# A two-layer encoder on one core: which pairs take seven products, what is loaded first, and how the last block ends

## The chip, the cores and the metric

The kernel runs on one core of one Trainium2 chip. The metric is device time in microseconds of one execution, the median of the runs.

## The reference, cut to what matters

Two layers. Each reads the RMS-normalised input through one input projection, runs grouped-query attention with a rotary embedding beside a bidirectional retention, gates both, and adds an output projection to the residual. A final RMSNorm follows.

```python
D_MODEL = 4096; SEQ = 256; DEPTH = 2
for l in range(DEPTH):
    h = rmsnorm(x, norm_w[l])
    proj = h @ w_in[l]                       # (256, 4096) @ (4096, 11264)
    aq, ak, av, ag, rq, rk, rv, rg = jnp.split(proj, SPLIT_POINTS, axis=-1)
...
    a_out = (jax.nn.silu(ag) * gqa_attention(aq, ak, av)).astype(x.dtype)
...
    r_out = (jax.nn.silu(rg.astype(jnp.float32)) * r).astype(x.dtype)
    x = x + jnp.concatenate([a_out, r_out], axis=-1) @ w_out[l]     # (256, 4096) @ (4096, 4096)
return rmsnorm(x, final_norm)
```

## The kernel before

**Blocks and pairs.** The two projections of each layer are cut into blocks of 1024 output columns: 11 blocks of w_in, then 4 of w_out, 15 a layer, numbered 0 to 29 over both. Blocks 11 to 14 and 26 to 29 are the w_out of the two layers. Within a block the 4096 inputs are taken as 16 pairs of 128-row tiles. Two rows of tokens (m = 0, 1) by two halves of columns is a 2x2 matrix product for each pair, and it is done either with eight plain products (EIGHT_PRODUCTS, L182) or with seven (SEVEN_PRODUCTS, L171, a Strassen-Winograd form). The products of all pairs gather in PSUM banks M1 to M7.

**Products.** Every fp32 operand is split in a high and a low part, and one product is three matmuls of 512 columns: high by high, low by high, high by low. Only pairs 0 and 1 of block 0 are multiplied as plain fp32 (NATIVE), since there the input isn't split yet.

**Parts.** A weight page (pair and letter A, T, B or U) is loaded by SP (tile wraw); ACT writes its high part (whi) and DVE its low part (wlo). For a pair with seven products DVE also makes two weight sums (wsum) and both engines split them (pages T and U). "Far" pages (FARS, L101) take another way: POOL's queue loads the high part (fhi), ACT negates it (flo), and a second, adding DMA makes the low part. The stationary operands are the activations' parts: x7h and x7l for pairs that have seven parts, x8h, x8l and x3 for the others.

**Which pairs.** sevens_of() (L207) gives the pairs with seven products of a block: those in SEVEN, and those in AFTER from a given block on. slots_of() (L236) writes out the products of each page; a T or U page of a pair with eight products has none. A pair that changes to seven between blocks is converted by sevenfold() (L1105).

**Order.** The order of pages on PE is written by hand in ORDERS (L87) for some blocks, else in_groups() (L218) makes it. The order on ACT, DVE, POOL and SP is made when the program is built, by a planner (pump, L1344, and aside, L1377) that picks by due times; SETS (L110) gives single blocks other slacks. Once built, each engine runs its own list in order.

**The start.** SP loads `small` (gains and decays), the half of x for pair 1 (tile `full`), two halves of pair 1's weights (`fhi`), and the other half of x. ACT scales x by the gains (split_pair, L998), first index 0, then 1. PE multiplies 20 times on zeros (warm, L2163) ahead of that.

**The end.** In the last block pair 15's products stand last, in the order M5, M2, M3, M4 (FINAL_ORDER), and M4 has 30 matmuls at the end, ten products of five pairs. last_combine() (L2059) adds the banks into `ca` and `cb` (two column blocks, rows m = 0 and 1), adds the residual (`res`, in tiles x8h and x8l), squares and sums. When a row's sum is there, POOL takes the power (tile `last`), ACT and DVE scale the eight column blocks of the row, and SP stores each (tile to `out`, 256 KB). Row 0 is done after M3, row 1 after M4.

## Time and profile before

| | |
|---|---|
| median of 3 runs | 2579.61 us (2579.35 to 2580.07) |
| the profiled execution, its own time | 2581.24 us |
| its span, first to last instruction | 2579.4 us |
| TensorE busy | 2565.5 us, 99% |
| VectorE busy | 2347.1 us, 91% |
| ScalarE busy | 1695.7 us, 66% |
| GpSimd busy | 461.3 us, 18% |
| DMA | 688.64 MB, mean 267 GB/s |

The profiled execution lies 1.63 us above the median, and 1.84 us of its time lie outside the span. Times below are us from the start of the span. PE is TensorE, DVE is VectorE, ACT is ScalarE, POOL is GpSimd, SPq is SyncE's queue. A matmul's own duration overlaps the next one; how far two starts lie apart is what it costs.

### The profile page before, as it was taken

The page shows a single profiled execution, that of the slowest core. Times are in us where ns is not written, and L with a number is a line of the kernel's source. Part 1 is how long each engine was busy: PE and PEld are TensorE (multiplying, and loading weights), DVE is VectorE, ACT ScalarE, POOL GpSimd, SP SyncE. Part 2 cuts the span into 40 slices and gives each one's busy share as a digit, 9 for nine tenths or more (in the row PEclk, how much of TensorE's full clock was granted, in tenths as well). Part 3 has the DMA queues.
Part 4 walks back from the last instruction along what each step waited for, and adds up shares of the span by engine and source line. Part 5 has one row for each costly group of instructions (what it writes and reads, how often), then busy time and mean ns, then how long its engine had stood idle before and what let it go on. Part 6 is the DMA issues. An engine that isn't in the chain of part 4 may idle for free.

```text
span 2579.4 us, 34271 instructions
## 1 busy us (share of the span) xinstructions
PE 2565.5 (99%) x11491; PEld 2124.7 (82%) x11491; DVE 2347.1 (91%) x2951; ACT 1695.7 (66%) x2439; POOL 461.3 (18%) x682
## 2 busy tenths in 40 slices
PE   9999999999999999999999999999999999999998
PEld 6888888888888888888888888888888888888886
DVE  7998998999989999888999998989999899998887
ACT  7766676666655668555786666776676566675565
POOL 0112221221111111221221112212211111111111
PEclk9999999999999999999999999999999999999999
DMA  9988988888778787998998889888987787888886
GB/s 329 318 265 267 290 260 271 287 273 254 228 237 263 226 287 236 294 279 245 326 310 261 270 260 298 276 258 284 275 264 232 239 254 239 276 245 265 265 269 204
DMA packets 198401, 688.64 MB, mean 267 GB/s; under 512 B 24272, under 2 KB 24400, under 8 KB 198224
## 3 DMA queue, kind: packets, MB, share of 16 engines
q1 hardware_dynamic: 126160, 445.24, 48.4%
q0 software_dynamic: 72064, 241.21, 37.1%
q8 instruction: 90, 1.47, 0.2%
q14 instruction: 87, 0.71, 0.1%
HBM read 639.17 MB, written 47.19 MB: 266 GB/s over the span
## 4 chain that ended last, share of the span: by engine, by line
PE 98%; DVE 1%; DMA 1%; issue 0%; ACT 0%; POOL 0%; POOLq 0%; DVEq 0%; SPq 0%; ACTq 0%
PE M L446 94%; PE ps L446 4%; DMA q<-q_dram 0%; DVE wlo L446 0%; DVE cb L446 0%; DMA full<-in_xT 0%; ACT ps L446 0%; DVE ca L446 0%; ACT whi L446 0%; ACT pTh L446 0%; ACT full L446 0%; DVE aql L446 0%; DVE sgT L446 0%; POOLq L2288 0%; DVE wsum L446 0%
## 5 line engine op out<-in xcount | busy, mean ns | idle before, releaser
L446 ACT CAST whi<-wraw 128x1024 fp32r<-128x1024 f32 (+1 forms) x811 | 756.5, 938 | 358.6 <-PE M L446 296.4
L446 DVE TENSOR_TENSOR wlo<-wraw,whi 128x1024 fp32r<-128x1024 f32 (+1 forms) x811 | 866.3, 1078 | 68.7 <-ACT whi L446 63.4
L446 ACT CAST whi<-wsum 128x1024 fp32r<-128x1024 f32 x406 | 426.2, 1050 | 252.7 <-PE M L446 122.2
L446 DVE TENSOR_TENSOR wlo<-wsum,whi 128x1024 fp32r<-128x1024 f32 x406 | 494.5, 1218 | 103.2 <-ACT whi L446 73.7
L446 PE MATMUL M<-whi,x7h 128*128 128x512 f32 x1465 | 570.7, 390 | 0.0
L446 PE MATMUL M<-whi,x7l 128*128 128x512 f32 x1465 | 570.4, 389 | 0.0
L446 PE MATMUL M<-wlo,x7h 128*128 128x512 f32 x1465 | 475.9, 389 | 0.0
L446 PE MATMUL M<-whi,x8l 128*128 128x512 f32 x1165 | 453.5, 389 | 0.0
L446 PE MATMUL M<-whi,x8h 128*128 128x512 f32 x1165 | 453.5, 389 | 0.0
L446 PE MATMUL M<-wlo,x8h 128*128 128x512 f32 x1165 | 359.7, 389 | 0.0
L446 PEld LDWEIGHTS M<-wlo,x7h 128*128 128x128 f32 x1465 | 275.1, 188 | 57.3
L446 PEld LDWEIGHTS M<-whi,x7l 128*128 128x128 f32 x1465 | 275.2, 188 | 56.4 <-issue 0.2
L446 PEld LDWEIGHTS M<-whi,x7h 128*128 128x128 f32 x1465 | 275.2, 188 | 56.3 <-issue 0.2
L446 PEld LDWEIGHTS M<-wlo,x8h 128*128 128x128 f32 x1165 | 218.7, 188 | 45.5
L446 PEld LDWEIGHTS M<-whi,x8h 128*128 128x128 f32 x1165 | 218.8, 188 | 45.2 <-DVE ca L446 0.2
L446 PEld LDWEIGHTS M<-whi,x8l 128*128 128x128 f32 x1165 | 218.8, 188 | 44.9
L446 ACT ACTIVATE flo<-fhi 128x1024 fp32r<-128x1024 f32 (+1 forms) x145 | 152.2, 1050 | 155.8 <-PE M L446 150.6
L446 DVE TENSOR_TENSOR wsum<-wraw 128x1024 f32<-128x1024 f32 x203 | 247.0, 1217 | 4.7 <-PE M L446 2.8
L446 PE MATMUL M<-whi,x 128*128 128x512 f32 x736 | 226.7, 389 | 0.0
L446 POOL DMA_DIRECT2D fhi<-in_w_in x106 | 58.8, 555 | 865.3 <-PE M L446 865.1
L446 PE MATMUL M<-fhi,x8l 128*128 128x512 f32 x429 | 167.0, 389 | 0.0
L446 PE MATMUL M<-fhi,x8h 128*128 128x512 f32 x429 | 167.0, 389 | 0.0
(266 smaller groups left out, 3172.4 us busy)
## 6 DMA issues: line engine op xcount, KB each, us to landing
wraw<-in_w_in SPq DMA_DIRECT2D x594, 512.0 KB, 5.9
wraw<-in_w_out SPq DMA_DIRECT2D x217, 512.0 KB, 6.3
fhi<-in_w_in POOLq DMA_DIRECT2D x106, 512.0 KB, 5.1
flo<-in_w_in POOLq DMA_DIRECT2D x106, 512.0 KB, 8.2
fhi<-in_w_out POOLq DMA_DIRECT2D x36, 512.0 KB, 4.7
flo<-in_w_out POOLq DMA_DIRECT2D x36, 512.0 KB, 8.3
full<-next_dram POOLq DMA_DIRECT2D x24, 512.0 KB, 7.6
p_dram<-room POOLq DMA_DIRECT2D x64, 128.0 KB, 5.2
```

Source lines behind the costliest of these rows:

```text
L446: op.call()
```

## The change

- SEVEN loses pair 2, and AFTER gains it: from block 0 on in the first layer's w_in and in both w_out, from the second block on in the second layer's w_in. So in block 15 pair 2 takes eight products where it took seven, and sevenfold() converts it for block 16.
- EXTRA is (4,). Neither SEVEN nor AFTER names pair 4, and sevens_of() reads nothing else, so pair 4 has eight products in every block, as before; the pages 4T and 4U in the new orders have no product. The code in sevenfold() that puts parts in the rotary tables' tile (`cs`) is there before and after and isn't reached.
- The hand-written orders of blocks 1, 6, 10, 11, 12, 15, 24, 26, 27, 28 and 29 differ in what they yield (blocks 1 and 15 fall back to in_groups()); of the other 19 blocks the order on PE is what it was. Blocks 0 and 12 have other far pages, three fewer in all. Some planner settings differ.
- At the start x goes ahead of `small`, and index 1 of x is scaled before index 0.
- In the last block row 0's additions go first. Row 1's M5 addition and its residual move behind M3. The last two products of M4 are done in two column halves, the second into a bank of its own ("rest"), with an addition and a square for each.

Over the whole program PE has 9 more matmuls: three of 512 columns, and twelve of 256 in the place of six of 512. DVE has 4 more instructions, ACT 1, SP 3 more loads of wraw, POOL 6 fewer DMAs.

SP, the start of the program. Before:

```order
L446 DMA small_97<-in_small 128x128
L446 DMA full_128<-in_xT 128x512
L446 DMA fhi_130<-in_w_in 128x512 x2
L446 DMA full_128<-in_xT 128x512
L446 DMA fhi_134<-in_w_in 128x1024
```

After:

```order
L458 DMA full_127<-in_xT 128x512
L458 DMA small_97<-in_small 128x128
L458 DMA fhi_130<-in_w_in 128x512 x2
L458 DMA full_127<-in_xT 128x512
L458 DMA fhi_134<-in_w_in 128x1024
```

`small` and the first half of x have changed places; the rest stands.

PE, first block of the second layer (15), pair 2: page A before (its pages T, B and U follow further on, 21 matmuls in all):

```order
L446 MATMUL M1_11721<-whi_11775,x7h_11436 128x512
L446 MATMUL M1_11721<-whi_11775,x7l_11437 128x512
L446 MATMUL M3_11737<-whi_11775,x7h_11436 128x512
L446 MATMUL M3_11737<-whi_11775,x7l_11437 128x512
L446 MATMUL M1_11721<-wlo_11782,x7h_11436 128x512
L446 MATMUL M3_11737<-wlo_11782,x7h_11436 128x512
```

Page A after (with page B, which follows, 24 matmuls):

```order
L458 MATMUL M3_11737<-whi_11787,x7h_11437 128x512
L458 MATMUL M3_11737<-whi_11787,x7l_11438 128x512
L458 MATMUL M5_11749<-whi_11787,x7h_11437 128x512
L458 MATMUL M5_11749<-whi_11787,x7l_11438 128x512
L458 MATMUL M4_11756<-whi_11787,x7h_11437 128x512
L458 MATMUL M4_11756<-whi_11787,x7l_11438 128x512
L458 MATMUL M2_11759<-whi_11787,x7h_11437 128x512
L458 MATMUL M2_11759<-whi_11787,x7l_11438 128x512
L458 MATMUL M3_11737<-wlo_11797,x7h_11437 128x512
L458 MATMUL M5_11749<-wlo_11797,x7h_11437 128x512
L458 MATMUL M4_11756<-wlo_11797,x7h_11437 128x512
L458 MATMUL M2_11759<-wlo_11797,x7h_11437 128x512
```

The pair feeds M3, M5, M4 and M2 in place of all seven banks, with three matmuls more.

DVE, the end of the last block, from the additions after bank M6 to the first scaling of an output. Before (x8h and x8l are the residual's rows 1 and 0; `last` is the sum of row 0):

```order
L446 TENSOR_TENSOR cb_23017<-ca_23016,x8h_22650 128x512
L446 TENSOR_TENSOR ca_23016<-ca_23016,x8h_22646 128x512
L446 TENSOR_TENSOR cb_23017<-cb_23017,x8l_22648 128x512
L446 TENSOR_TENSOR ca_23016<-ca_23016,x8l_22644 128x512
L446 TENSOR_TENSOR cb_23017<-cb_23017,M5_22470 128x512 x2
L446 TENSOR_TENSOR ca_23016<-ca_23016,M2_22482 128x512
L446 TENSOR_TENSOR cb_23017<-cb_23017,M3_22459 128x512
L446 TENSOR_REDUCE last_23111<-sums_20250 128x1
L446 TENSOR_SCALAR last_23111<-last_23111 128x1
L446 TENSOR_SCALAR cb_20978<-cb_20978,last_23111 128x512
```

After:

```order
L458 TENSOR_TENSOR cb_23033<-cb_23033,x8l_22625 128x512
L458 TENSOR_TENSOR ca_23032<-ca_23032,x8l_22621 128x512
L458 TENSOR_TENSOR cb_23033<-cb_23033,M5_22464 128x512
L458 TENSOR_TENSOR ca_23032<-ca_23032,M2_22491 128x512
L458 TENSOR_TENSOR cb_23033<-cb_23033,M3_22458 128x512
L458 TENSOR_TENSOR cb_23033<-ca_23032,M5_22464 128x512
L458 TENSOR_REDUCE last_23098<-sums_20249 128x1
L458 TENSOR_SCALAR last_23098<-last_23098 128x1
L458 TENSOR_TENSOR cb_23033<-cb_23033,x8h_22627 128x512
L458 TENSOR_TENSOR ca_23032<-ca_23032,x8h_22623 128x512
L458 TENSOR_SCALAR cb_20975<-cb_20975,last_23098 128x512
```

Two residual additions and one of the two M5 additions have moved behind M3; the two residual additions now stand between row 0's mean and its first scaling.

The diff, cut to its core (of the tables a line or two):

```diff
--- before.py
+++ after.py
@@ -66,13 +66,13 @@
-SEVEN = (0, 2, 5, 8, 11, 13)
+SEVEN = (0, 5, 8, 11, 13)
...
-AFTER = ({10: (3, 1)}, {10: (1, 1)})
-EXTRA = ()
+AFTER = ({2: (0, 1), 10: (3, 1)}, {2: (0, 0), 10: (1, 1)})
+EXTRA = (4,)
@@ -85,34 +85,42 @@
 ORDERS = {
...
-    12: '0A 0T 1A 0B 1B 0U 2A 3A 2T 3B 2B 4A 2U 4B 5A 6A 5T 6B 5B 7A 5U 7B 8A 9A 8T 9B 8B 8U 10A 10T 10B 10U 11A 12A 11T 12B 11B 11U 13A 14A 13T 14B 13B 13U 15A 15B',
...
+    12: '0A 0T 1A 1B 0B 0U 2A 3A 2T 3B 2B 2U 4A 4T 4B 5A 4U 6A 5T 6B 5B 7A 5U 7B 8A 9A 8T 9B 8B 8U 10A 10T 10B 10U 11A 12A 11T 12B 11B 11U 13A 14A 13T 14B 13B 13U 15A 15B',
...
 FARS = {
-    0: '3B 9B 12B 15B 7A',
+    0: '3B 15B 10A',
...
 SETS = {
-    (0, 'PE_REST'): 6.0,
+    (0, 'PE_REST'): 2.0,
...
+    (6, 'PE_REST'): 4.0,
...
-    (10, 'SOFT'): 5.0,
+    (11, 'PE_REST'): 4.0,
+    (11, 'SLACK'): 1.0,
...
+    (27, 'REST'): 4.0,
@@ -249,6 +257,10 @@
+LAST_SOME = NB // 2
+LAST_ENTRIES = 2
@@ -637,7 +649,6 @@
-    sy.dma_start(small, small_in)
@@ -778,13 +789,15 @@
-        def load_whole(self, n):
+        def load_whole(self, n, k=ALL):
...
+            if k == 0:
+                sy.dma_start(g.raw[:, 0, :], g.src[0][:, 0, :])
+                return
...
-            for k in (1, 0) if n == 0 else (ALL,):
-                sy.dma_start(g.raw[:, k, :], g.src[0][:, k, :])
+            sy.dma_start(g.raw[:, k, :], g.src[0][:, k, :])
@@ -1004,7 +1017,7 @@
         if gains:
-            for i in range(2):
+            for i in (1, 0):
@@ -1847,7 +1860,7 @@
         def combining():
-            for _ in range(len(first)):
+            for _ in range(len(first) + last):
                 while not events:
@@ -1919,10 +1932,11 @@
-        def multiply(name, a, b, start, stop):
+        def multiply(name, a, b, start, stop, cols=ALL):
...
+            b, to = b[:, cols], acc[name][:, cols]
...
-            op.e, op.ins, op.outs, op.dma = "P", ins, [region(acc[name])], None
+            op.e, op.ins, op.outs, op.dma = "P", ins, [region(to)], None
@@ -1930,7 +1944,7 @@
-            pe.matmul(acc[name], a, b, start=start, stop=stop)
+            pe.matmul(to, a, b, start=start, stop=stop)
@@ -1948,10 +1962,10 @@
-        n = 0
-        while n < len(flat):
+        n, until = 0, len(flat) - (LAST_ENTRIES if last else 0)
+        while n < until:
             group = [(n, *flat[n])]
-            while n + len(group) < len(flat) and (flat[n + len(group)][1], flat[n + len(group)][3]) == (flat[n][1], flat[n][3]) and len(group) < TOGETHER:
+            while n + len(group) < until and (flat[n + len(group)][1], flat[n + len(group)][3]) == (flat[n][1], flat[n][3]) and len(group) < TOGETHER:
@@ -1975,6 +1989,21 @@
             n += len(group)
+        end = [(m, *flat[m]) for m in range(until, len(flat))]
+        end = [(m, p, k, h, stationary(p, index), prepare(name, p, index, k, h)) for m, name, p, index, k, h in end]
+        if end:
+            acc["rest"] = t(pm, [P, NB], "M1")
+        for name, cols in (("M4", slice(0, LAST_SOME)), ("rest", slice(LAST_SOME, NB))) if end else ():
+            for i, (m, p, k, h, a, g) in enumerate(end):
+                final_one = i == len(end) - 1
+                for j in range(2):
+                    multiply(name, a[j], g.hi[h], name == "rest" and not i and not j, False, cols)
+                stall(lambda: g.lo is not None and g.added)
+                multiply(name, a[0], g.lo[h], False, final_one, cols)
+            if name == "M4":
+                events.append("M4 some")
+        for m, p, k, _, _, _ in end:
+            ended(m, "M4", p, k)
...
     def combine(bank, acc, c):
@@ -2058,14 +2087,38 @@
-        room = []
-        def square(m, c, i):
+        room, r = [], {}
+        some = slice(0, LAST_SOME)
+        rest = slice(LAST_SOME, NB)
+        def square(m, c, i, cols=ALL, to=None):
...
-            ac.activation(room[0], c[i][:, m, :], AF.Square, accum_out=sums[:, m, n : n + 1])
+            to = sums[:, m, n : n + 1] if to is None else to
+            ac.activation(room[0][:, cols], c[i][:, m, cols], AF.Square, accum_out=to)
+        def finish(m):
+            for n, engine in ((0, ac), (1, ve), (2, ac), (3, ve), (5, ve), (4, ac), (6, ve), (7, ve)):
+                v = outs[n][:, m, :]
+                if n >= N_OUT - 2:
+                    ve.scalar_tensor_tensor(v, v, r[m], fn[n - N_OUT + 2], op0=ALU.mult, op1=ALU.mult)
+                elif engine is ve:
+                    ve.tensor_scalar_mul(v, v, r[m])
+                else:
+                    ac.activation(v, v, AF.Copy, scale=r[m])
+                one = Lane(iter(()))
+                before, active[0] = active[0], one
+                sy.dma_start(out[m * P : (m + 1) * P, columns(n)], v)
+                active[0] = before
+                do(partial(lanes.append, one))
+        def mean(m):
+            v = t(sp, [P, 1], "last", 2)
+            ve.tensor_reduce(v, sums[:, m, :N_OUT], axis=AX.X, op=ALU.add)
+            ve.tensor_scalar(v, v, 1.0 / D_MODEL, EPS, op0=ALU.mult, op1=ALU.add)
+            return v
...
         def last(bank, acc, c):
@@ -2074,8 +2127,6 @@
             ca, cb = c
             if bank == "M6":
                 combine(bank, acc, c)
-                ve.tensor_add(cb[:, 1, :], ca[:, 1, :], res[1, 1])
-                ve.tensor_add(ca[:, 1, :], ca[:, 1, :], res[0, 1])
...
             elif bank == "M2":
@@ -2083,45 +2134,29 @@
             elif bank == "M5":
...
-                ve.tensor_add(cb[:, 1, :], cb[:, 1, :], acc["M5"])
-                square(1, c, 1)
             elif bank == "M3":
                 combine(bank, acc, c)
...
-                r[0] = last_rstd(0)
-                for n, e in ((0, ac), (1, ve), (2, ac), (3, ve), (5, ve), (4, ac), (6, ve), (7, ve)):
-                    finish(0, n, e)
+                ve.tensor_add(cb[:, 1, :], ca[:, 1, :], acc["M5"])
+                r[0] = mean(0)
+                gp.tensor_tensor(r[0], r[0], half[:, :1], op=ALU.pow)
+                ve.tensor_add(cb[:, 1, :], cb[:, 1, :], res[1, 1])
+                ve.tensor_add(ca[:, 1, :], ca[:, 1, :], res[0, 1])
+                square(1, c, 1)
+                finish(0)
+            elif bank == "M4 some":
+                ve.tensor_add(ca[:, 1, :], ca[:, 1, :], acc["M4"])
+                square(1, c, 0, some)
             elif bank == "M4":
-                combine(bank, acc, c)
-                square(1, c, 0)
-                r[1] = last_rstd(1)
-                for n, e in ((0, ac), (1, ve), (2, ac), (3, ve), (5, ve), (4, ac), (6, ve), (7, ve)):
-                    finish(1, n, e)
-        r = {}
-        def finish(m, n, engine):
-            v = outs[n][:, m, :]
-            if n >= N_OUT - 2:
-                ve.scalar_tensor_tensor(v, v, r[m], fn[n - N_OUT + 2], op0=ALU.mult, op1=ALU.mult)
-            elif engine is ve:
-                ve.tensor_scalar_mul(v, v, r[m])
-            else:
-                ac.activation(v, v, AF.Copy, scale=r[m])
-            one = Lane(iter(()))
-            before, active[0] = active[0], one
-            sy.dma_start(out[m * P : (m + 1) * P, columns(n)], v)
-            active[0] = before
-            do(partial(lanes.append, one))
+                more = t(sp, [P, 8], "rs", 3)[:, :1]
+                ve.tensor_add(ca[:, 1, rest], ca[:, 1, rest], acc["rest"][:, rest])
+                square(1, c, 0, rest, more)
+                r[1] = mean(1)
+                ve.scalar_tensor_tensor(r[1], more, 1.0 / D_MODEL, r[1], op0=ALU.mult, op1=ALU.add)
+                gp.tensor_tensor(r[1], r[1], half[:, :1], op=ALU.pow)
+                finish(1)
...
-    def last_rstd(m):
-        r = t(sp, [P, 1], "last", 2)
-        ve.tensor_reduce(r, sums[:, m, :N_OUT], axis=AX.X, op=ALU.add)
-        rsqrt(r, r, 1, D_MODEL)
-        return r
@@ -2154,11 +2189,15 @@
-        step = KG * SEQ // (2 if c == 0 else 1)
-        for k in reversed(range(0, KG * SEQ, step)):
-            sy.dma_start(full[c][:, k : k + step], xT[c, :, k : k + step])
-            if c == 0 and k:
-                weights.load_whole(0)
+        if c:
+            sy.dma_start(full[c], xT[c])
+            return
+        for v in (slice(2 * SEQ, 4 * SEQ), slice(0, 2 * SEQ)):
+            sy.dma_start(full[c][:, v], xT[c, :, v])
+            if v.start:
+                sy.dma_start(small, small_in)
+                for k in (1, 0):
+                    weights.load_whole(0, k)
```

## Rows read from the trace of the kernel before

**Rows 1.** The page: busy time of the engines, share of the span, instructions.

```profile
PE 2565.5 (99%) x11491; PEld 2124.7 (82%) x11491; DVE 2347.1 (91%) x2951; ACT 1695.7 (66%) x2439; POOL 461.3 (18%) x682
```

**Rows 2.** All that PE waited for: us in total, times, longest.

```profile
PE ps L446 <- DVE junk L446: 1.1, 1, 1.1
PE ps L446 <- DVE aql L446: 0.7, 1, 0.7
PE M L446 <- ACT full L446: 0.6, 1, 0.6
```

**Rows 3.** The chain in two stretches: start us, us, matmuls in one go.

```profile
1998.54 134.21 PE M L446 x592
2132.75 0.71 PE ps L446 x6
```

**Rows 4.** Timeline of PE at an attention product: start us, us, form.

```profile
428.23 0.40 PE L446 MATMUL ps<-kv,aqh 128*128 128x256 f32 x2
...
430.18 0.40 PE L446 MATMUL M<-whi,x8h 128*128 128x512 f32 x1
```

**Rows 5.** Timeline of DVE and PE at a retention product near 2258 us.

```profile
2256.61 1.41 DVE L446 SCALAR_TENSOR_TENSOR vl<-cb,rstd,vh 128x512 fp32r<-128x512 f32 x2
...
2258.26 0.28 PE L446 MATMUL ps<-vl,wTh 128*128 128x256 f32 x1
```

**Rows 6.** Busy time by stretch: most of block 15.

```profile
core 0: us, PE busy (x) PEld busy (x) DVE busy (x) ACT busy (x) POOL busy (x), PEclk, DMA share, GB/s
1291.20:1375.00 83.80, 83.80 (x371) 69.44 (x370) 83.30 (x132) 63.99 (x105) 18.11 (x27) 1.00 0.92 290
```

**Rows 7.** The chain at the start of the program.

```profile
1.19 3.89 DMA full<-in_xT
...
5.17 0.92 ACT full L446 x2
...
6.13 2.08 PE M L446 x2
```

**Rows 8.** Tile fhi up to 9 us: its loads, from issue to landing.

```profile
L446 SPq DMA_DIRECT2D fhi<-in_w_in x3: 424/432/432, 1.7 to 3.1; - x3
...
DMA to landing us min/median/max: 4.1/4.3/5.9
```

**Rows 9.** Timeline of PE's weight loads (PEld) in the first products.

```profile
8.85 0.34 PEld L446 LDWEIGHTS M<-fhi,full 128*128 128x128 f32 x1 [0.52 <-issue]
...
10.52 0.19 PEld L446 LDWEIGHTS M<-fhi,full 128*128 128x128 f32 x1 [0.48 <-issue]
```

**Rows 10.** Timeline of DVE, ACT and POOL in the last block, row 0.

```profile
2556.84 0.69 DVE L446 TENSOR_TENSOR cb<-ca,M 128x512 f32<-128x512 f32 x1 [2.35 <-PE M L446]
...
2562.62 0.68 DVE L446 TENSOR_TENSOR cb<-cb,M 128x512 f32<-128x512 f32 x1
...
2563.65 0.60 ACT L446 ACTIVATE ps<-cb 128x512 f32<-128x512 f32 x1
...
2564.41 0.16 DVE L446 TENSOR_REDUCE last<-sums 128x1 f32<-128x8 f32 x1 [1.11 <-ACT ps L446]
...
2565.45 1.28 DVE L446 TENSOR_SCALAR cb<-cb,last 128x512 f32<-128x512 f32 x3 [0.69 <-POOL last L446]
```

**Rows 11.** Timeline of PE in the last block: M3's last matmul, the program's last.

```profile
2560.72 0.39 PE L446 MATMUL M<-flo,x 128*128 128x512 f32 x1
...
2567.52 0.39 PE L446 MATMUL M<-x7h,x8h 128*128 128x512 f32 x1
```

**Rows 12.** Timeline of SP's queue and DVE: first store, row 1's additions and scaling.

```profile
2565.96 0.34 SPq L446 DMA_DIRECT2D out<-cb  x1
...
2567.97 0.68 DVE L446 TENSOR_TENSOR ca<-ca,M 128x512 f32<-128x512 f32 x1
...
2570.51 1.28 DVE L446 TENSOR_SCALAR cb<-cb,last 128x512 f32<-128x512 f32 x3 [0.67 <-POOL last L446]
```

**Rows 13.** DMA from 2564.0 us to the end, in 40 slices of 0.385 us.

```profile
GB/s 0 0 0 0 0 0 0 271 378 383 378 388 357 404 367 404 362 383 388 367 394 367 399 367 399 367 399 367 388 378 383 383 388 372 394 319 0 0 0 0
```

More of the change, by code (lines that the diff above doesn't have):

```diff
@@ L106 @@
     11: '3B 6B 12B 15B',
+    12: '3B 6B 12B 15B',
     24: '3B 9B 12B 15B',
```

12 rows, old and new, of the table ORDERS are left out of this document.

## The prediction

> **What bounds the kernel now.** I read the page's first part before anything else: TensorE is busy for 99% of the span, VectorE for 91%, nothing else for over 66% [rows 1]. Then the list of all that PE waited for, to see what a new order could still save: three waits, 1.1 us before its warming-up products, 0.7 us at an attention product, 0.6 us at the first real product [rows 2]. Then the chain, to see what a matmul costs: 592 matmuls of 512 columns in 134.21 us, 0.2267 us each, and six attention products of 256 columns in 0.71 us, 0.118 us each [rows 3]. So the time is the sum of PE's list, plus a start of 6.13 us before the first real product, plus what follows PE's last matmul (2567.52 + 0.39 = 2567.91) up to 2579.4. A change can win a microsecond or two at the two ends; in between it wins only by taking matmuls out.
>
> How dear a wait is shows at 428 us: two products start at 428.23 and the next block's first at 430.18; the six attention products between took 1.95 us where 0.71 is their price, so 1.24 us were lost in all, of which the list of waits names 0.7 [rows 2 to 4]. VectorE has places with little room: in most of block 15 it is busy for 83.30 of 83.80 us [rows 6].
>
> **Pair 4.** EXTRA and the pages 4T and 4U in the new orders look as if pair 4 should take seven products in w_out. The code doesn't do that: sevens_of() reads SEVEN and AFTER, and neither names pair 4; EXTRA alone does. The pages 4T and 4U of the new orders are empty. PE's list has 9 matmuls more and not fewer. Cost and gain: 0.
>
> **Pair 2.** In block 15 alone it takes eight products for seven: three more matmuls of 512 columns, 3 x 0.2267 = **+0.68 us**, on PE and so on the path. In exchange VectorE is spared the two weight sums of that pair, and sevenfold() gives it the splits for block 16. Outside the last block it has two instructions more in the whole program, so the 0.50 us that it had free in that stretch [rows 6] stays about as it was.
>
> **The new page orders.** The same products in another order cost PE nothing, unless a page's weights come late. Eleven blocks are concerned, block 15 among them. I set each part's end against the first matmul that reads it at its new place; by this, one place goes below zero. Near 2258 us the retention product starts 0.24 us after VectorE's last part for it is done (2256.61 + 1.41 = 2258.02, start 2258.26) [rows 5]; it now stands three matmuls (0.68 us) further ahead: **+0.44 us** if VectorE's list doesn't move. Lower bound for this term: -1.24, if by a shift of all that lies ahead of it the wait at 428 us goes, though no row of that place is changed. Upper bound: 0.44 and two waits like that one, 0.44 + 2 x 1.24 = 2.92.
>
> **The start.** x is issued at 1.19 and lands 3.89 us later, ACT's two scalings take 0.92, and PE starts at 6.13 [rows 7]. With x issued ahead of `small` (0.45 us earlier) the scalings could end at about 5.6. But the first weights aren't there then: their first load is issued at 1.7 and the fastest took 4.1, so 5.8 [rows 8]. That is 0.33 us. `small` now goes second and ACT needs it too; it is the smaller of the two and is issued where x was, so I let it be hidden by the same 3.89; if it weren't, the gain is nothing. The products up to 10.5 us run at the lower of TensorE's two levels, 1.2 GHz: a weight load takes 0.34 us at 8.85 and 0.19 us at 10.52 [rows 9]. If the level rises at the same time whatever the start, only half of the 0.33 is won. I take **-0.2 us**, bounds 0 and -0.45 (the whole issue).
> The Trainium skill, page "TensorE: Matmul & The Clock Gate", section "Part 1: The HAM clock gate (the "warmup" mystery)", says that the moment of the rise itself varies by 500 ns to either side from run to run. By that alone an execution would move by up to a quarter of a microsecond, and one profile couldn't tell the gain at the start from it. No row here shows this spread.
>
> **The end.** Sixteen stores of 256 KB leave at 357 to 404 GB/s with no gap from 2566.7 to 2577.8 [rows 13]: at 380 GB/s 0.69 us each. The first is issued at 2565.96, 0.51 us after VectorE's first scaling at 2565.45; row 1's first scaling is at 2570.51 [rows 10, 12], 5.06 us later, while row 0's eight stores need 8 x 0.69 = 5.52. So row 1 waits for the queue by 0.46 us, and what sets the end is when row 0's first scaling starts.
> Row 0 today: M3's last matmul ends at 2560.72 + 0.39 = 2561.11 [rows 11], but its addition starts only at 2562.62, since VectorE has been adding without a pause from 2556.84 on, 0.60 us each. The last square ends at 2563.65 + 0.60, the sum starts at 2564.41, and after POOL's power the scaling starts at 2565.45, 1.04 us after the sum [rows 10].
> After: three additions ahead of M3's are gone (3 x 0.60 = 1.8 us), so M3's starts at 2561.2, right behind its matmul. The square follows without row 1's ahead of it, its sum at about 2562.7, the power ready at 2562.7 + 1.04 = 2563.7. Here the new thing that is late: two residual additions now stand between the mean and the scaling on VectorE, and with row 1's M5 addition (2561.8 to 2562.4) they run from 2563.05 to 2564.3. The first scaling: 2564.3, **1.15 us earlier**. ACT squares row 1 in the same time and is free at about 2564.6.
> Row 1 today: M4's addition at 2567.97 (0.68), scaling 2.54 us after [rows 12]. After: half of it is added and squared ahead; the other half, 256 columns, saves about 0.3 us of the addition and 0.25 of the square, and pays 0.06 for twelve short matmuls (12 x 0.118 - 6 x 0.2267) and some 0.15 for one more tiny instruction (the mean's took as much as the sum's, 0.16). Scaling at about 2570.0 to 2570.1, 0.4 to 0.5 earlier. Row 0's stores end 1.15 us earlier, row 1's start 0.5 earlier: the slack of 0.46 is used up and the queue stands for some 0.1 to 0.2 us. Gain **-1.0 us**, bounds 0 (the additions cost what they spare) and -1.2.
> The Trainium skill, page "DMA: Bandwidth & Descriptors", section "Where 436 GB/s comes from", gives 435 GB/s as the fabric's ceiling and about 358 as the limit where HBM is one side; the row's 380 lies between. By 435, as an estimate, a store would take 0.60 us, the queue would have no backlog, and the end would gain row 1's 0.5 only. The measured rate decides.
>
> **Sum.** +0.68 + 0.44 - 0.2 - 1.0 = -0.08 us. On the profiled execution 2581.24 becomes 2581.16; that execution lies 1.63 us above the median, and I take the same distance off: 2579.5.
>
> **Rivals.** (a) *The end gives nothing*: the two residual additions and row 1's square hold VectorE and ACT as long as before. For: both stand ahead of the scalings now. Against: three additions went away in exchange [rows 10]. 0.68 + 0.44 - 0.2 = +0.9: 2580.5. (b) *Slower: the new orders make PE wait.* The mechanism is that of 428 us, a page's part that VectorE delivers late, 1.24 us each time [rows 4]. For: VectorE had only 0.50 us free in 83.80 [rows 6]. Against: in the whole kernel before one such wait is left [rows 2]. It decides from five waits on: 5 x 1.24 = 6.2, and 0.68 - 0.2 - 1.0 beside it, +5.7, 2585.3; one in each of the eleven blocks gives +13.1, 2592.7. (c) *The lower level lasts longer*: with an earlier start or a gap at the start, the stretch from 6.13 to 10.5 [rows 7, 9] is run through once more at half the rate, 4.4 / 2 = +2.2: 2581.7. (d) *Pair 4 does take seven after all*, against the reading above: eight blocks x 3 x 0.2267 = -5.4: 2574.1.
>
> **How the numbers follow.** Forecast 0.65 (2579.5); (a) 0.20; (b) 0.08; (c) 0.05; (d) 0.02. The measurement can tell 0.2%, 5.2 us. Faster by more: (d) alone, 0.02. Slower by more: (b) from five waits on, 0.07. The rest, 0.91, is within. The range goes by the bounds of the four terms: low 0.68 - 1.24 - 0.45 - 1.2 = -2.2, 2577.4; high 0.68 + 2.92 = +3.6, 2583.2. It holds the forecast, (a) and (c).
>
> **What would show it.** Right: the list of PE's waits still three or four rows, none over 1 us but the first; 11500 matmuls; first real product at 5.8 to 6.0; M3's addition at about 1.4 us less than before relative to the last matmul; the stores a block with at most one short gap. Wrong: new rows of waits of PE on wlo, whi or flo in blocks 1, 6, 10 to 12, 15, 24 or 26 to 29; fewer than 11491 matmuls; a store queue that starts no earlier against PE's last matmul.

## The result, and the profile after

| | before | after |
|---|---|---|
| median of 15 runs | 2579.11 us (2577.89 to 2581.01) | 2583.71 us (2580.53 to 2588.02) |
| after / before | | 1.0018, 95% interval 1.001 to 1.0026 |
| profiled execution, its own time | 2581.24 us | 2587.41 us |
| its span | 2579.4 us | 2585.6 us |

The changed kernel is slower by 4.6 us, a little under the 0.2% that was set as the bound for "same", and 0.5 us above the forecast range. Three of its fifteen runs took 2587.4 to 2588.0 us and the other twelve 2580.5 to 2585.1; the profiled execution is one of the three, 3.7 us above the median, so its trace shows the bad case and not the usual one.

The page's first part of the changed kernel, busy time and instructions of each engine (before: [rows 1]):

```profile
PE 2568.8 (99%) x11500; PEld 2124.4 (82%) x11500; DVE 2350.5 (91%) x2955; ACT 1699.7 (66%) x2441; POOL 459.1 (18%) x676
```

The nine matmuls more are there, so pair 4 has kept its eight products. What is new stands in the list of what PE waited for, here the five longest of nine rows (before: [rows 2], three rows in all):

```profile
PE M L458 <- DMA flo<-in_w_in: 3.1, 1, 3.1
PE ps L458 <- DVE junk L458: 1.1, 1, 1.1
PE M L458 <- DVE wlo L458: 0.6, 1, 0.6
PE M L458 <- ACT x8h L458: 0.4, 1, 0.4
PE M L458 <- DMA flo<-in_w_out: 0.4, 1, 0.4
```

The largest is a transfer: flo, the low part of a far page. Its place is block 15; the timeline of PE there (start, us, form):

```profile
1325.83 0.39 PE L458 MATMUL M<-fhi,x8l 128*128 128x512 f32 x1
1329.29 1.12 PE L458 MATMUL M<-flo,x8h 128*128 128x512 f32 x2 [3.07 <-DMA flo<-in_w_in]
1330.21 0.63 PE L458 MATMUL M<-flo,x 128*128 128x512 f32 x1
1330.63 0.63 PE L458 MATMUL M<-flo,x8h 128*128 128x512 f32 x1
```

The next matmul starts 3.46 us after the last one where 0.23 is the price. And behind the gap the matmuls start 0.43 us apart, not 0.2267, up to about 1332.8. In the table of stretches, whose third number from the end is the granted TensorE clock, that is

```profile
1326.00:1333.00 7.00, 3.93 (x10) 2.94 (x10) 6.35 (x17) 2.11 (x3) 0.90 (x2) 0.76 1.03 410
```

a mean of 0.76 for a stretch in which PE first stood and then ran at the lower of its two levels, 1.2 GHz. One wait of 3.2 us for a late transfer has so cost 5.0 us in all. Comparing the starts of PE's matmuls with their prices, further losses that the trace of before doesn't have lie near 37 us (0.8), at 614 to 619 us (1.2, at the end of block 6), at 1077 us (0.7, a flo in block 12) and at 1910 us (0.3).

**The end.** M3's last matmul on PE, then VectorE in the last block, as in [rows 10 to 12]:

```profile
2568.09 0.39 PE L458 MATMUL M<-flo,x 128*128 128x512 f32 x1
```

```profile
2568.51 0.69 DVE L458 TENSOR_TENSOR cb<-cb,M 128x512 f32<-128x512 f32 x1 [0.37 <-PE M L458]
...
2571.52 1.28 DVE L458 TENSOR_SCALAR cb<-cb,last 128x512 f32<-128x512 f32 x3
...
2577.37 1.28 DVE L458 TENSOR_SCALAR cb<-cb,last 128x512 f32<-128x512 f32 x3 [0.68 <-POOL last L458]
```

M3's last matmul starts at 2568.09 here and at 2560.72 before [rows 11]. Measured from it, M3's addition comes 0.42 us later (before 1.90), row 0's first scaling 3.43 (before 4.73) and row 1's 9.28 (before 9.79). So row 0 is 1.30 us earlier and row 1 0.51. The DMA traffic from 2566 us to the end, in 40 slices of 0.49 us (before: [rows 13]), shows the short gap between the two rows' stores (the slices at 299 and 213 lack some 0.3 us of the full rate):

```profile
GB/s 0 0 0 0 0 0 0 0 0 0 0 0 0 90 389 377 365 393 377 389 377 377 381 381 299 213 365 393 377 381 393 389 373 356 401 381 172 0 0 0
```

### The profile page after: what moved, and what is told of

It is laid out like the page before. It is cut to its first block, busy times and chain, and to the rows that moved or that the text cites. A ratio compares the mean times of both kernels' runs of the same rounds, so it can differ in the third digit from the quotient of the medians.

```text
span 2585.6 us, 34283 instructions
## 1 busy us (share of the span) xinstructions
PE 2568.8 (99%) x11500; PEld 2124.4 (82%) x11500; DVE 2350.5 (91%) x2955; ACT 1699.7 (66%) x2441; POOL 459.1 (18%) x676
## 4 chain that ended last, share of the span: by engine, by line
PE 95%; DMA 3%; DVE 1%; issue 1%; ACT 0%; SPq 0%; POOL 0%; POOLq 0%; DVEq 0%; ACTq 0%
PE M L458 91%; PE ps L458 4%; DMA wraw<-in_w_in 1%; DMA flo<-in_w_out 1%; DMA flo<-in_w_in 0%; DMA wsum<-in_w_in 0%; DVE wlo L458 0%; SPq L458 0%; DVE wsum L458 0%; DVE cb L458 0%; ACT whi L458 0%; DVE ca L458 0%; ACT flo L458 0%; POOL last L458 0%; ACT full L458 0%
## 5 line engine op out<-in xcount | busy, mean ns | idle before, releaser
L458 PEld LDWEIGHTS M<-whi,x 128*128 128x128 f32 x738 | 138.5, 188 | 29.2 <-ACT whi L458 0.5
```

What stands on the lines that cost most here:

```text
L458: op.call()
```

## The experiments

All times are medians of 11 runs, each beside 33 runs of the kernel before on the same chip (2578.52, 2578.60 and 2578.55 us on the three chips). The ratio and its interval stand in brackets; the ratio is not that of the two medians and can differ from it (experiment 10: 2.09 us by the medians, 1.3 by the ratio). Where the interval holds 1, in experiments 1, 4, 5, 6, 10 and 11, the times alone leave it open whether anything has changed, and the reading rests on the trace.

**1. The code alone.** The tables SEVEN, AFTER, EXTRA, ORDERS, FARS and SETS are those of before, the code is the changed one.

> The kernel before with the changed code alone (x first, row 0's additions first, last products halved); SEVEN, AFTER, ORDERS, FARS and SETS are those of before. In the changed kernel's trace TensorE had lost 11.9 us at 50 us against 12.3 before (0.3 us won at the start), and its last matmul started 10.5 us before the end of the span against 11.9. Theory A (the whole loss lies in the moved pages): this kernel is 1.2 to 2.4 us faster than before, ratio 0.9991 to 0.9995, and its list of waits of PE is that of before. Theory B (the two ends lose as well): no faster than before, or slower.

Measured: 2578.76 us, +0.24 (ratio 1.0001, 0.9992 to 1.001). By the time this is theory B, but the two ends do not both lose: the end has its gain in the trace (PE's last matmul starts 10.7 us before the end of the span, 11.9 in the kernel before), yet the time is that of before. So something in the code costs about what the end gives. PE's list of waits has a candidate: 0.9 us on `fhi`, at the start, where the kernel before has none.

**2. Block 15 alone.**

```diff
-SEVEN = (0, 2, 5, 8, 11, 13)
+SEVEN = (0, 5, 8, 11, 13)
-AFTER = ({10: (3, 1)}, {10: (1, 1)})
+AFTER = ({2: (0, 1), 10: (3, 1)}, {2: (0, 0), 10: (1, 1)})
-    15: '0A 0T 1A 1B 0B 0U 2A 3A 2T 3B 2B 4A 2U ...',
```

> The kernel before with pair 2 of block 15 in eight products for seven (and that block's order as in the changed kernel) and nothing else. Theory A (one late low part of a far page in block 15, flo, with a stretch at the lower clock behind it, is the largest loss): 3 to 6 us slower than before, of it 0.68 for three matmuls; the list of waits of PE gets a row on flo of w_in near 1325 us of 1 to 3.5 us. Theory B (the loss is spread over many re-ordered blocks, VectorE late): 0.7 to 1.0 us slower, no row on flo.

Measured: 2580.63 us, +2.11 (1.0011, 1.0002 to 1.002); nine runs from 2579.3 to 2582.0, two at 2585.8. The last of the three rows of its list of waits, and the landing of the flo that PE waited for:

```profile
PE M L445 <- DMA flo<-in_w_in: 0.8, 1, 0.8
```

```profile
DMA to landing us min/median/max: 9.0/9.0/9.0
```

The row on flo is there, smaller than in the changed kernel's profile, and no lowered clock behind it in this execution. Theory A holds in kind; its 3 to 6 us are above the median. The transfer itself was not slow here: it landed in 9.0 us, against 8.6 in the kernel before. It was issued late, 4.8 us after PE's last product on the flo before (2.9 in the kernel before, 4.8 in the changed one).

**3. All but block 15.** The changed kernel with `AFTER[0]` naming pair 2 as (0, 0) and block 15's old order.

> The changed kernel with pair 2 of block 15 back in seven products and that block in its old order. Theory A: 3 to 6 us less than the changed kernel, so 0 to 2 us below the kernel before; no wait on flo near 1325 us. Theory B: only the 0.7 us of three matmuls less than the changed kernel, so some 4 us above the kernel before.

Measured: 2580.59 us, +2.07 (1.001, 1.0001 to 1.0018). No wait at 1325 us. By the medians block 15 is half of the loss; the other half is elsewhere, more than theory A had left for it. Experiments 2 and 3 together make 4.2 of the 4.6 us.

**4. Pair 4 with seven products.**

```diff
-AFTER = ({2: (0, 1), 10: (3, 1)}, {2: (0, 0), 10: (1, 1)})
+AFTER = ({2: (0, 1), 10: (3, 1)}, {2: (0, 0), 4: (1, 1), 10: (1, 1)})
```

> The changed kernel with pair 4 named in AFTER for w_out from the second block on, so that six blocks take seven products for it (18 matmuls of 512 columns fewer, four conversions' worth of work more for VectorE and ScalarE at the first block's end of each w_out). By the matmuls alone 18 x 0.2267 = 4.1 us less than the changed kernel. Theory A: the wait on flo in block 15 stays as it is, so about the time of the kernel before (within 2 us). A rival: VectorE, which has the new weight sums to make, is late in w_out and takes it back: no faster than the changed kernel, new rows of waits on wlo or wsum in blocks 12 to 14 and 27 to 29.

Measured: 2577.93 us, -0.59 (0.9993, 0.9985 to 1.0002), 5.8 us less than the changed kernel by the medians and 5.2 by the distances to the kernel before. 11482 matmuls, 18 fewer. In this kernel POOL's list around block 15 is another one, and its trace has no wait on flo at all, in block 12 or 15. The wait went although block 15's products were not touched; experiment 9 follows this up.

**5. The start alone.**

```diff
-    sy.dma_start(small, small_in)
...
-            for i in range(2):
+            for i in (1, 0):
...
-        for k in reversed(range(0, KG * SEQ, step)):
-            sy.dma_start(full[c][:, k : k + step], xT[c, :, k : k + step])
+        for v in (slice(2 * SEQ, 4 * SEQ), slice(0, 2 * SEQ)):
+            sy.dma_start(full[c][:, v], xT[c, :, v])
+            if v.start:
+                sy.dma_start(small, small_in)
```

> The kernel before with the changed start alone (x ahead of small, index 1 of x scaled first). The profile of the changed code alone shows the first real product at 5.47 us and the first product on split weights at 21.00; that of block 15 alone, which has the old start, shows 6.51 and 19.94. Theory A (the new start delivers the second half of x and the later weights later, so that PE starts earlier and stands behind): 0.8 to 1.6 us slower than before, the first product on split weights at about 21 and a second gap of PE near 37 us. Theory B (the start gains what the prediction said): 0.2 to 0.5 us faster, no gap near 37 us.

Measured: 2580.00 us, +1.40 (1.0006, 0.9997 to 1.0015); 5 of the 11 runs lie above all 33 of the kernel before. The profiled execution is the slowest of the 11 (2584.0 us). PE's timeline at the start, this kernel first, then that of experiment 6, which has the old start:

```profile
5.34 1.10 PE L446 MATMUL M<-fhi,full 128*128 128x512 f32 x2 [0.31 <-DMA fhi<-in_w_in]
6.27 1.02 PE L446 MATMUL ps<-fhi,full 128*128 128x512 f32 x2
8.58 1.95 PE L446 MATMUL M<-fhi,full 128*128 128x512 f32 x4 [1.29 <-DMA fhi<-in_w_in]
11.04 1.13 PE L446 MATMUL M<-fhi,full 128*128 128x512 f32 x2 [0.51 <-DMA fhi<-in_w_in]
```

```profile
5.80 1.12 PE L450 MATMUL M<-fhi,full 128*128 128x512 f32 x2 [0.53 <-ACT full L450]
6.76 1.02 PE L450 MATMUL ps<-fhi,full 128*128 128x512 f32 x2
7.62 2.74 PE L450 MATMUL M<-fhi,full 128*128 128x512 f32 x6
```

With the new start PE begins 0.46 us earlier and then stands twice for the weights. The three loads of fhi (issue to landing, min, median, max), new and old start:

```profile
DMA to landing us min/median/max: 3.6/6.3/7.9
```

```profile
DMA to landing us min/median/max: 4.0/4.2/5.6
```

They are issued at the same moments. The first lands no later, the second 2.1 and the third 2.3 us later. This execution is the extreme: over the seven traces with either start the second load takes 4.7 to 6.3 us with the new one and 4.0 to 4.7 with the old, the third 6.5 to 7.9 and 5.5 to 6.0. The first product on split weights starts at 21.9 us here and at 19.2 there (20.5 to 21.0 and 19.1 to 20.0 in the other profiles with the one and the other start, 21.7 in that of before, whose clock rose late). Theory A holds for the size and for these landings; the second gap that it expected near 37 us is not in this trace, and experiment 12, with the old start, has one of 0.5 us there. Why the loads land later when `small` stands behind x and not ahead of it was not tried apart; it stays open.

**6. The end alone.** The kernel before with only last_combine() and the halved products of the changed one.

> The kernel before with the changed end alone. In the three profiles with the new end PE's last matmul starts 10.54 to 10.73 us before the end of the span against 11.85 to 11.87 in the two with the old one; with 0.17 off for a last matmul of half the size, about 1.0 to 1.15 us are won. Theory A: 0.9 to 1.2 us faster than before, and with the start's loss this makes the changed code's zero. Theory B (the new end's gain is taken back by something that only the median shows): no difference from before.

Measured: 2577.63 us, -0.97 (0.9996, 0.9987 to 1.0004); 8 of the 11 runs lie below all 33 of the kernel before. PE's last matmul starts 10.7 us before the end of the span, 11.9 in the kernel before. Theory A. With experiment 5: +1.40 - 0.97 = +0.43, where the code alone measured +0.24.

**7. A wider stretch in block 15.** One line is added to the changed kernel's ORDERS:

```diff
+    15: '0A 0T 1A 1B 0B 2A 0U 3A 3B 2B 4A 4B 5A 6A 5T 6B ...',
```

> The changed kernel, block 15 still with eight products for pair 2, but with page 3B two pages' work earlier there (2A 0U 3A 3B 2B in place of 2A 0U 2B 3A 3B): the stretch between the last low product of page 3B, which frees the only flo buffer, and the first of page 6B grows by 2.7 us, from 12.9 to 15.6 us; the products are the same in number. Theory A (that stretch is too short for ACT's negation, the adding transfer and its landing): no wait on flo near 1325 us, the median 1 to 2.5 us below that of the changed kernel, and no runs 4 to 5 us above its median. Theory C (pair 2's eight products bring VectorE or the loads behind as such): the wait stays, the time stays.

Measured: 2582.70 us, +4.10 (1.0019, 1.001 to 1.0028), one run at 2589.9. Its list of waits still has

```profile
PE M L459 <- DMA flo<-in_w_in: 1.2, 1, 1.2
```

although the stretch did grow: the last product on the first flo starts at 1309.82, that on the next would have stood at 1325.5. The flo issued at 1313.46 took this long to land:

```profile
DMA to landing us min/median/max: 13.3/13.3/13.3
```

So theory A as I had put it, that the stretch alone is too short, does not come out: the wait is 1.2 in place of 3.1 us with 2.7 us more of stretch, because this flo lands 2.0 us later than that of the changed kernel, and the median is only 0.5 us nearer to the kernel before. Theory C isn't shown by it either: what differs is the landing.

**8. The kernel before, squeezed.**

```diff
-    15: '0A 0T 1A 1B 0B 0U 2A 3A 2T 3B 2B 4A 2U 4B 5A ...',
+    15: '0A 0T 1A 1B 0B 0U 2A 3A 2T 2B 2U 3B 4A 4B 5A ...',
```

> The kernel before, pair 2 of block 15 with its seven products, but page 3B behind 2U there: the stretch from the last low product of 3B to the first of 6B shrinks by about 2 us, to some 12.9 us, as in the changed kernel; no product more or less. Theory A: a wait on flo of w_in near 1325 us of 0.5 to 3.5 us and 1 to 3 us slower than before, with single runs 4 to 6 us slower. Theory C: as fast as before.

Measured: 2580.95 us, +2.35 (1.001, 1.0001 to 1.0018). Slower as expected, but not where I expected it: no wait at 1325 us, where flo landed in 8.0 us and the shorter stretch was enough. The wait is on another flo, at 1449 us in block 16:

```profile
PE M L446 <- DMA flo<-in_w_in: 1.1, 1, 1.1
```

It was issued at 1438.49 and took

```profile
DMA to landing us min/median/max: 12.3/12.3/12.3
```

where the kernel before has 9.1 for that page. No product had been added or taken; a page had moved, and with it POOL's list in the blocks behind: two stores (kv_dram<-k) were issued 2.0 and 0.7 us ahead of this flo. In these two traces, then, the landing is the longer term (13.3 and 12.3 us); in experiment 2 it was the late issue.

**9. flo ahead in POOL's queue.** The order of the products is untouched; in block 15 the planner holds POOL's other work back (holds(), not shown here, is true from the moment PE begins a far page until the next page's flo is issued):

```diff
-                while v.ops and v.ops[0].e in "GS" and model.begins(v.ops[0]) <= at + 0.05:
+                while v.ops and v.ops[0].e in "GS" and not (v.ops[0].e == "G" and holds()) and model.begins(v.ops[0]) <= at + 0.05:
```

> The changed kernel with every product where it was; only in block 15 POOL's list holds the other transfers and the power of rstd back from the moment PE begins a far page until the next page's flo is issued. So flo stands ahead of ca<-in_x at the first far page and ahead of next_dram and rstd at the second, as in the kernel before. The landing of flo took 13.7 and 11.3 us at these two in the changed kernel, 9.3 and 8.6 before. Theory A (what flo stands behind in POOL's queue makes it late): landings of 8 to 10 us, no wait on flo near 1325 us, median 1 to 2 us below the changed kernel's, no runs 4 to 5 us above the median. Theory C (eight products in that block as such: the stretch between two far pages, or the load): the wait stays.

Measured: 2581.86 us, +3.31 (1.001, 1.0001 to 1.0019), against +4.60 for the changed kernel; no run above 2583.6. The two intervals overlap, so the 1.3 us between them are not clear of noise; the trace tells more. POOL's timeline in the changed kernel, then in this one:

```profile
1307.94 2.22 POOL L458 DMA_DIRECT2D next_dram<-room  x4 [1.82 <-DVE room L458]
1312.92 0.56 POOL L458 DMA_DIRECT2D fhi<-in_w_in  x1 [2.75 <-PE M L458]
1317.15 0.81 POOL L458 TENSOR_TENSOR rstd<-rstd,half 128x2 f32<-128x2 f32 x1 [3.67 <-DVE rstd L458]
1317.93 0.91 POOL L458 DMA_DIRECT2D flo<-in_w_in  x1
```

```profile
1312.43 0.53 POOL L458 DMA_DIRECT2D fhi<-in_w_in  x1 [5.11 <-PE M L458]
1314.44 0.88 POOL L458 DMA_DIRECT2D flo<-in_w_in  x1 [1.48 <-ACT flo L458]
1315.00 2.56 POOL L458 DMA_DIRECT2D next_dram<-room  x4
```

In the changed kernel four small stores and the power of rstd, for which POOL itself waits 3.67 us, stand ahead of flo, which goes out at 1317.93; here at 1314.44. That is 4.8 us after PE's last product on the flo before has started there (1313.14), and 1.8 us here (1312.65). The rstd is the smaller part of this. The holding back has changed ACT's list as well: in the changed kernel the negation that makes the first half of flo stands behind two squares of the residual, which wait for a transfer of POOL's queue themselves,

```profile
1315.01 0.63 ACT L458 ACTIVATE room<-cb 128x512 f32<-128x512 f32 x1 [0.47 <-DMA cb<-in_x]
...
1316.26 1.04 ACT L458 ACTIVATE flo<-fhi 128x1024 fp32r<-128x1024 f32 x1
```

and here it starts at 1313.08, as soon as PE has left the buffer. The landings of the first and the second flo of block 15, changed kernel and this one:

```profile
DMA to landing us min/median/max: 13.7/13.7/13.7
...
DMA to landing us min/median/max: 11.3/11.3/11.3
```

```profile
DMA to landing us min/median/max: 7.6/7.6/7.6
...
DMA to landing us min/median/max: 8.5/8.5/8.5
```

PE's list of waits has no row on flo any more. So theory A holds in another form than the stretch: the wait goes when flo is put first, at its negation on ACT, at its issue and in its landing, with all products where they were. Of the 5.8 us won from PE's leaving the buffer to the landing, 3.0 are the earlier issue and 2.8 the shorter landing; by this sum either alone would have taken most of the wait of 3.2, which was not tried. The Trainium skill, page "DMA: Bandwidth & Descriptors", section "SWDGE vs HWDGE vs iDMA", says that a single queue is there for all transfers that GpSimd issues; the landings agree, 13.7 us at the first flo with ca<-in_x just ahead of it and 7.6 with that behind. Over all traces it took 13.4 to 13.7 us in the three with ca<-in_x ahead of it, 7.4 to 9.3 in the eleven others. What stands ahead is not all of it: at the second flo the four stores stood ahead in three traces, and it took 9.0, 11.3 and 13.3 us.

**10. Block 6 alone.**

```diff
-    6: '0A 0T 1A 1B 0B 0U 2A 3A 2T 3B 2B 6A 4A 2U 4B 5A 5T ...',
+    6: '0A 0T 1A 1B 3A 0B 0U 2A 2T 3B 2B 4A 2U 4B 5A 6A 5T ...',
...
+    (6, 'PE_REST'): 4.0,
```

> The kernel before with the changed order of block 6 (page 3A moved up ahead of 0B, 6A and 4A exchanged with it) and its PE_REST of 4.0, nothing else. The changed kernel less block 15 is 1.8 us slower than the changed code alone; its profile shows waits at 614 to 618 us (2.2 us), at 1079 us (0.8 us) and near 37 us. Theory A (the block boundary behind block 6, where PE waits for the additions into ca and cb): 0.7 to 1.5 us slower than before, gaps of PE at 613 to 617 us. Theory B (those waits come of the later start, not of block 6): as fast as before.

Measured: 2580.64 us, +2.09 (1.0005, 0.9996 to 1.0014). The gaps are where expected, 0.7 us before 613.5 and 0.4 before 615.4. The chain that ends there, in order of time:

```profile
598.20 10.90 DMA wraw<-in_w_in
609.10 0.02 issue
609.12 1.23 DVE wsum L447
...
612.77 0.61 DVE ca L447
```

A page loaded by SP lands after 10.9 us; the weight sum waits for it; the additions into cb and ca, which free the banks for the next block, stand behind that sum on VectorE; PE waits for ca. With the old order of the block (experiment 6) no chain leads away from PE in this stretch. Theory A holds for the place. For the size the trace, of the median run, has some 1.5 us there with the slower matmuls behind the gaps; the median of +2.09 lies above the 0.7 to 1.5 expected, and the interval does not tell it from 1.5 or from nothing. Why wraw lands late there isn't told by the trace: its loads took 10.9 us in the median from 595 to 612 us, 6.8 with the old order.

**11. Block 12 alone.**

```diff
-    12: '0A 0T 1A 0B 1B 0U 2A 3A 2T 3B 2B 4A 2U 4B 5A 6A ...',
+    12: '0A 0T 1A 1B 0B 0U 2A 3A 2T 3B 2B 2U 4A 4T 4B 5A 4U 6A ...',
...
+    12: '3B 6B 12B 15B',
```

> The kernel before with the changed order of block 12 (1B ahead of 0B, 2U ahead of 4A) and its far pages without 9B, nothing else. Theory A (as in block 15: flo stands behind four next_dram transfers in POOL's queue and lands after 13.7 us in place of 9.9): 0.4 to 0.9 us slower than before, one wait on flo of w_out near 1075 us, its landing 13 to 14 us. Rival: no difference, no wait.

Measured: 2579.59 us, +1.04 (1.0004, 0.9995 to 1.0012). Inconclusive. The profile fell on its fastest run, 2577.66 us, and has no wait at 1075 us; its flo took 12.3 us to land, in the changed kernel 13.7, before 9.9, and here that was just early enough. The landing is longer as expected; that the wait makes the 1 us is not shown.

**12. The end and pair 4, without the rest.** The kernel before with the new end and with pair 4 in seven products as in experiment 4; the start and blocks 0, 1, 6, 15 and 24 are the old ones, blocks 10 to 12 and 26 to 29 have the changed orders.

> The kernel before with the changed end, and with pair 4 in seven products in six blocks of w_out (with the changed orders of blocks 10 to 12 and 26 to 29, which place its pages 4T and 4U); the start and blocks 0, 1, 6, 15 and 24 are those of before. From the runs: the end alone is worth -1.0 us; the changed kernel with pair 4 is 5.2 us below the changed kernel where 18 matmuls of 512 columns explain 4.1. Theory A (the parts add up): 4.5 to 6 us faster than before, ratio 0.9977 to 0.9983. Rival (VectorE is late in w_out without the other changes): less than 3 us faster, waits on wlo or wsum in blocks 12 to 14 or 27 to 29.

Measured: 2573.62 us, **-4.93** (0.998, 0.9971 to 0.9989); all 11 runs lie below all 33 of the kernel before. The page and all that PE waited for:

```profile
PE 2560.1 (100%) x11479; PEld 2120.2 (82%) x11479; DVE 2373.2 (92%) x3000; ACT 1705.6 (66%) x2459; POOL 460.2 (18%) x680
```

```profile
PE ps L458 <- DVE junk L458: 1.1, 1, 1.1
PE ps L458 <- DVE aql L458: 0.7, 1, 0.7
PE M L458 <- DVE wlo L458: 0.4, 1, 0.4
PE M L458 <- ACT full L458: 0.2, 1, 0.2
```

18 x 0.2267 = 4.1 for the matmuls and 1.0 for the end make 5.1. The parts add up, and VectorE carries 26 us more while PE waits only 0.4 us more for it: the first two rows stand in the list of the kernel before as well. The changed order of block 12 is in this kernel too: its flo landed in 6.8 us and PE did not wait for it, so that order by itself does not cost the 1 us. This version beats both kernels, by 4.9 and by 9.5 us.

## Why the prediction was wrong, step by step

**What bounds the kernel** held: PE's list plus the two ends. It is the reason why every part is so small, and why the forecast of no gain was near. The range failed because it was built from places that had been looked at.

**Pair 4: right.** The new EXTRA does nothing without AFTER (11500 matmuls). What it would have brought was near in size: rival (d) said 5.4 us for eight blocks, which is 4.1 for six, and that experiment 12 bears out. That experiment 4 gave 5.2 is in part luck, since the waits on flo went there too.

**Pair 2: right as far as it went.** Three matmuls, 0.68 us. Block 15 alone costs 2.11 (by its interval 0.5 to 5); the other 1.4 were not in the sum.

**The new page orders: the step that failed.** I set the ends of the weights' parts against their first use, and took VectorE for the one engine that could be late: +0.44 near 2258 us. The trace of after has no gap there. The three gaps that it has in re-ordered blocks, 6, 12 and 15, begin with a DMA: SP's wraw in block 6, POOL's flo in the others. For flo my margin kept the issue and the landing of before and moved only PE. But the change also reorders POOL's list, and with it ACT's, and there is only one flo buffer: the negation can't begin before PE has left the last far page, so in the trace of before four flos of blocks 12, 15 and 16 are issued 11.8 to 15.9 us ahead of their use, and a late one can be made good only out of that. In block 12, with 13.2 us from issue to use, a landing of 9.9 us fits and one of 13.7 doesn't. Two rows that were to be had of the trace of before would have shown it: the landings of flo, 8.6 and 9.3 us at the two pages of block 15, against 12.06 us from issue to use at the second. That is 3.5 us of room, on a queue that I hadn't followed. In the changed kernel's profiled execution three things take it away at this page: PE comes to it 2.0 us sooner after its last product on the flo before (12.9 us in place of 15.0; this is the order of the eight products), flo goes out 1.9 us later (4.8 us after that product in place of 2.9), and it lands 2.7 us later (11.3 in place of 8.6). Together they are 6.6, which is 3.1 over the room, and the wait is 3.2. In experiment 2 they are 2.0, 1.9 and 0.4, 0.8 over the room, and PE waits 0.8. Only the first was in reach of my margin, and alone it would have left 1.4 us of room. The upper bound of two waits, 2.92 us, had no price for a longer one either: the wait of 3.2 us was followed by 1.75 us lost at the lower level, 1.2 GHz.

**The start: wrong in sign.** Forecast -0.2, bounds 0 and -0.45; measured +1.40. PE did start earlier, as the step said. But the step ended at PE's first product. The second and third load of weights land later with the new start, PE catches up with them and stands, and by the first product on split weights it is behind: 20.5 to 21.9 us in seven traces, against 19.1 to 20.0 in six of the seven with the old start. The range of this term had no loss in it, and I gave no reason that excluded one. With 1.40 in the place of its bound of 0 the upper end of the range would have been 2584.6, which holds the measured time. And the trace of before misled me here: in that execution PE stayed at 1.2 GHz till 10.5 us [rows 9] (the weight loads show it; the granted clock in the table of stretches reads 1.00 from 6.0 to 10.5 us), and I priced the gain at half. In the old start of experiment 6 the matmuls follow each other every 0.43 us from 6.76 on at the latest, the price at 2.4 GHz. The execution of before reaches the first product on split weights at 21.7 us, the other six with the old start at 19.1 to 20.0. The Trainium skill, page "TensorE: Matmul & The Clock Gate", section "Part 1: The HAM clock gate (the "warmup" mystery)", gives 500 ns to either side for the rise; between these executions it is over 3 us.

**The end: right.** Forecast -1.0, measured -0.97. M3's addition was to come 1.4 us earlier against PE's matmuls and comes 1.48; row 0's scaling 1.15 and comes 1.30; row 1's 0.4 to 0.5 and comes 0.51. The gap in the store queue is where it was to be, some 0.3 us where 0.1 to 0.2 was said. The interval of experiment 6 holds 1, so it is the trace that bears this term out.

**The rivals.** (b) is what happened, with another carrier and price: waits of re-ordered pages, of 0.5 to 3.2 us, that begin with a late transfer, in block 6 by way of VectorE. It had 0.08. It decides not only from five waits on, as I wrote, since one of 3.2 us counts for four. (a) and (c) did not happen, though a late lower level did, in block 15.

**The sum in measured terms:** start +1.40, end -0.97, block 15 +2.11, block 6 +2.09, block 12 +1.04 make +5.7, where the changed kernel has +4.6. By the intervals each term has some 2.3 us to either side. All but block 15 measured +2.07, where the terms make 3.6. Whether the terms overlap or are only measured too large stays open: at the end of block 6 PE loses 0.9 to 2.4 us in the five traces with the new order and the new start, some 1.5 in experiment 10 with the old start. Blocks 0, 1 and 24 were not tried alone.

## What to carry to other kernels

When a change moves instructions, follow every queue's own order, the one that issues transfers first of all: what stands ahead of a transfer on its queue bears on when it goes out and when it lands, and a buffer that exists once leaves little room to make it up. A start that is earlier by half a microsecond is worth nothing if the stream behind it isn't; price the moment when the pipeline is full, not the first product. Where parts of a change are independent, as here, time them apart: one part of this one was a gain of 1.0 us, another, once it is really switched on, of some 4, and the other parts cost more than the first brought.

## What the runs showed of the hardware that I had not expected

- An adding transfer of 512 KB from POOL's queue landed 8.2 us after its issue in the median of the kernel before. At one far page of block 12 (near 1064 us) and the first two of block 15, over the 14 traces, it took 9.0 to 13.8 us in the eleven cases where ca<-in_x or four stores of next_dram stood unfinished ahead of it in that queue, and 6.8 to 10.0 us in the 31 others.
- A stand of 3.2 us in the middle of the kernel was followed by PE's lower level, 1.2 GHz: matmuls 0.43 us apart for some 3.4 us, 1.75 us on top. It was seen once. Behind the waits of 0.6 to 1.4 us only the first matmul or two were slower, by 0.1 us each.
- At the start, PE reached the higher level, 2.4 GHz, over 3 us later in one execution (before, at 10.5 us) than in another with the same start (experiment 6, by 6.8 us at the latest).
